# Where the modulation sums of a hybrid encoder layer are worked: all of them ahead of the mLSTM stage

## The chip, the cores and the metric

The kernel runs on one core of a Trainium2 chip. The metric is the device time of one execution in microseconds (us). The core's engines work side by side, each through its own instructions in a fixed order: PE (TensorE, the matrix engine), DVE (VectorE), ACT (ScalarE), POOL (GpSimd) and SP (SyncE), which here does nothing but issue transfers (DMAs). An instruction whose input is not ready holds up all that stand behind it on the same engine.

## The reference, cut to what matters

The input is `x` (1024 positions of 1024 numbers, float32) and a conditioning vector `c`. One layer is computed:

```python
cond = jax.nn.silu(c)
mod = cond @ w_ada + b_ada                  # 6 x 1024 numbers
sh1, sc1, g1, sh2, sc2, g2 = jnp.split(mod, 6, axis=-1)
h = modulate(rms_norm(x, norm_mix_g), sh1, sc1)
proj = h @ w_in                             # q, k, v of the attention; q|k, v, o, gates of the mLSTM
y_attn = axial_gqa_attention(...)           # 8 heads of 64, 2 key/value heads, axial rope on q and k
y_mem = bidirectional_mlstm(...)            # 4 heads of 128, depthwise convolution on q|k, chunked scan both ways
x = x + g1 * (jnp.concatenate([y_attn, y_mem], -1) @ w_out)
h = modulate(rms_norm(x, norm_ffn_g), sh2, sc2)
x = x + g2 * ((silu(h @ w_gate) * (h @ w_up)) @ w_down)
return rms_norm(x, final_norm_g)
```

The matrix products with the weights are kept close to float32: each operand is split into a rounded part ("hi") and a rest ("lo"), and a product is three matmuls, hi*hi, hi*lo and lo*hi.

## The kernel before

**Stages.** In order of time: the load of `x` and the first part of `mod`; the first columns of the input projection; the attention; the mLSTM; the output projection; the feed-forward network (FFN). The tiles have 128 partitions. A product of the input projection has an output of 128x512 or 128x256 that is summed over eight k-tiles of three matmuls each (`mm3`, lines 323 to 325: `acc` for feature-major outputs, `acct` for token-major ones).

**What sets the order.** The program is written out by a planner at build time. `Clock` holds a modelled time, `Engine` adds a modelled cost for every instruction, `ck.chain` runs a list of steps each when the one before is modelled as done, and `Flag` marks an event. `ck.streams(mains, fills, stop)` puts the next ready piece of the main streams on PE, and where none is ready a piece of the fill. During the attention the mains are `scores`, `turned` and `values`, and the fill is the rest of the input projection (`IN`). During the mLSTM the mains are `ends`, `backs`, `fronts` and `all_states`; the fill is first what is left of `IN`, then `MIX`, the output projection: 16 units "o" that read the attention's result (`ya_d`) and 16 units "m" that read the mLSTM's. A unit is 12 matmuls of 128x512 (`acc<-yah`, `yal`). With it come one split of a weight on ACT and DVE (`whi`, `wlo`) and one addition onto `x` on DVE (`x<-acc,mod,x`).

**The modulation sums.** `mod` has 48 columns, each a sum over `w_ada` times `cond`. The first 16 are worked at the start. For the other 32, `ada_late` loads half a column tile at a time (128x512, 64 halves in all, two tiles in turn) and sums it. Halves 0 to 47 are worked in the attention: `scores` calls `ada_late` once a round, the product is made on POOL and the sum on ACT (`ada<-ada,cond`, then `ada,modacc<-ada`). Halves 48 to 63 are worked in the mLSTM stage, where `ck.tick` calls `ada_late` ahead of each piece: product and sum in one instruction on DVE. For these `cond` is loaded and put through its activation a second time (`load_cond`), since the pool that held it has been closed. The list `summed` says that all 64 are added into `mod`. The streams of the first part of the mLSTM stage stop only when the fill `IN` has run out, its outputs are stored and `summed` is set; only then is the pool of `x1` opened, are the rows of `x` loaded, and does `MIX` become the fill.

**The ropes.** `rope_steps` takes one tile of q or k through its normalisation (`ms`, lines 798 and 805), a swap of partitions by four transfers (`sw`), and the rotation. Calls 4 (the keys), 0 and 1 come first; call 1 is the third. `rope_ok[i]` is set when tile i is stored. The keys' rope waits for `rope_ok[0]` and `rope_ok[1]` before its last step. The attention begins (`ready`) when tile 3 is stored and the gates are through.

**Raw weights.** `load_piece` takes the next piece of weights. `piece` sends its load ahead; how far ahead is 2 (`AHEAD`) in part of the list and 0 in the rest.

Of the kernel before, what the change touches and what calls it, by code (L numbers as in the profile page):

```python
# [15 lines left out]
OP = mybir.AluOpType  # L16
# [244 lines left out]
def layer_kernel(ctx, tc, xT, c, w_ada, vecs, cons, rope, w_f, w_fT, w_t0, w_t, w_o, w_gu, w_d, out):  # L261
# [114 lines left out]
    with tc.manual_schedule():  # L376
# [122 lines left out]
        def load_piece():  # L499

            i = len(pieces)
            if i == len(specs):
                return
            while len(made) <= min(i + (AHEAD if i + AHEAD >= start["down"] or start["q", 2] <= i < start["f", 4] else 0), len(specs) - 1):
                piece(len(made))
            p, there, st = made[i]
            pieces.append(p)
            if isinstance(specs[i][0], str):
                set_piece(p, *specs[i][1])
                return  # L510
            split(p, 0.0, lambda: st[0], [P, *specs[i][1:3]], there,
                  lo=dve if i >= start["down"] or i < 12 or start["o", 0] <= i < start["b", 1] else None)
# [247 lines left out]
        def rope_steps(i, accs, raw=None, qg=None):  # L760
# [18 lines left out]
            def rooted(n):  # L779
                dve.tensor_mul(qg[:, halves(n)], accs[n][0], rstd[n])  # L780
                accs[n][1].set(ck, ck.fin + LAT)
# [6 lines left out]
            def swap():  # L788
                sw = X["sw"] = bp.tile([P, S], F32, tag="big", name="sw")
                for b in range(4):  # L790
                    arrive = dma(sw[32 * b:32 * b + 32], qg[32 * (b ^ 1):32 * (b ^ 1) + 32])
                ck.chain(arrive, rp_ok, lambda: dve.tensor_mul(sw, sw, rp[1]), lambda: dve.tensor_mul(qg, qg, rp[0]),
                         lambda: dve.tensor_add(qg, qg, sw), *((*rs_ok, *rope_ok[0:2]) if is_k else ()), finish, store)

# [41 lines left out]
            if raw is None:  # L836
                ck.chain(0.0, lambda: evac(0), lambda: evac(1), swap,
                         *[(slot("ms"), lambda n=n: squares(n)) for n in range(NH if is_k else 1)])
            else:
                ck.chain(0.0, rstd_ok[0], lambda: rooted(0), rstd_ok[1], lambda: rooted(1), shift_ok,  # L840
                         shifted, swap,
                         *[(slot("ms"), lambda n=n: squares(n)) for n in range(NH if is_k else 1)])
# [288 lines left out]
        adas = []  # L1131
        summed = []

        def ada_late(last=48, ahead=2):

            n = len(adas)
            if n == 64 and all(f.done for f in adas[-2:]) and not summed:
                summed.append(1)
                mod_sum(40, 48)
            if n >= last or n >= ahead and not (adas[n - ahead].done and adas[n - ahead].t <= ck.t):  # L1140
                return
            j, i = 16 + n // 2, n % 2
            t = PP["ada"].tile([P, HALF], F32, tag="ada", name="ada", bufs=ahead)
            if n < 48:
                adas.append(ck.chain(dma(t, w_ada[j][:, halves(i)]), lambda: gps.tensor_mul(t, t, PP["cond"][:, halves(i)]),
                                     lambda: act.activation(t, t, AF.Copy, accum_out=modacc[:, i, j:j + 1]),
                                     bg=["gps", "act"]))
                return
            adas.append(ck.chain(dma(t, w_ada[j][:, halves(i)]), lambda: dve.scalar_tensor_tensor(
                t, t, 1.0, PP["cond"][:, halves(i)], op0=OP.mult, op1=OP.mult, accum_out=modacc[:, i, j:j + 1])))  # L1150

# [49 lines left out]
        def turned():  # L1201

            for it in range(NQ // 2):
                for i in range(2):
                    q = 2 * it + i
                    for b in range(2):
# [14 lines left out]
                        if b == 1:  # L1221
                            Tem[q].set(ck, ck.t)

        def values():
# [978 lines left out]
        def ready():  # L2203
            return rope_ok[3].done and logf_ok.done and not open_sum[0]

        ck.streams([un], stop=ready)
        ck.need(*k2_ok, *va_ok)
        stpool.__exit__(None, None, None)
# [6 lines left out]
        ck.streams([un], stop=lambda: convs[-1].done and len(convs) == 8 and not open_sum[0])  # L2215
        while len(adas) < 48:
            ck.need(*adas[-2:])
            ada_late()
# [9 lines left out]
        def mod_sum(a, b):  # L2228
            dve.tensor_add(mod[:, a:b], modacc[:, 0, a:b], V("b_ada", a, b - a))
            dve.tensor_add(mod[:, a:b], mod[:, a:b], modacc[:, 1, a:b])  # L2230

        mod_sum(16, 40)
        sc2 = const.tile([P, KT], F32, name="sc2")
# [11 lines left out]
        load_q(0)  # L2245
        load_cond(bp)
        loaded = [Flag() for _ in range(MH)]
# [3 lines left out]
        mem = [Stream(g) for g in (ends(), backs(), fronts(), all_states())]  # L2251
        ck.tick = lambda: all(f.done for f in heads[0]["in"]) and ada_late(64)
        ck.streams(mem, [un], stop=lambda: un.wait is None and all(f.done for v in vo_ok for f in v) and summed)
        while not summed:
            ck.need(*adas[-2:])
            ada_late(64)
        ck.tick = None
        BIGP[0].__exit__(None, None, None)
# [115 lines left out]
```

## Time and profile before

| | us |
|---|---|
| median of 3 runs (1345.16 to 1345.59) | 1345.42 |
| the profiled execution | 1345.81 |
| its span on the core | 1344.0 |
| PE busy in it | 1276.7 |
| DVE busy in it | 1049.8 |

The span is 1.8 us shorter than the execution's own time; that part lies around the program. By the timeline the attention's first scores are followed by the last product of values at 490.8 us, the mLSTM's first matmuls stand at about 500 us, the first matmul of the output projection at 560.7 us, the mLSTM's last transposes at 624.2 us, and the first matmul of the FFN at 684.5 us. To read the views: "busy" is the time in which an engine had at least one instruction running; PEclk is the clock granted to PE as a share of the full one; a number in square brackets is the time the engine stood idle just before the instruction, and what ended it.

### The profile page before, as it was taken

The numbers are of one execution on the slowest core, as the hardware profiler recorded it, in microseconds if no ns is written. First come the engines' busy times: TensorE is split into PE (matmuls) and PEld (weight loads), VectorE is DVE, ScalarE is ACT, GpSimd is POOL, SyncE is SP. The second block draws the span as 40 slices with busy tenths as digits, with TensorE's granted clock in tenths as the row PEclk, the third lists the DMA queues.
The fourth block names the chain that finished last, engine by engine and source line by source line (L and its number), as shares of the span: only waits on it lengthen the run. The fifth ranks groups of instructions, "written<-read, shape, count | busy, mean of one in ns | idle before, by whom it ended". The sixth has DMA issues, their size and how long they took to land.

```text
span 1344.0 us, 19732 instructions
## 1 busy us (share of the span) xinstructions
PE 1276.7 (95%) x6656; PEld 1080.6 (80%) x6656; DVE 1049.8 (78%) x1694; ACT 707.0 (53%) x1338; POOL 527.7 (39%) x449
## 2 busy tenths in 40 slices
PE   9998898999999998899999999999999999999997
PEld 7887777888888897677878788888888887788886
DVE  7956698778898747997689989867767655888886
ACT  6583566687777756464477432333233333454452
POOL 0071577466676426442135155545454530000002
PEclk9997999899999999999999999999999999999999
DMA  9545433233333226753563344332233258933315
GB/s 374 198 121 141 118 101 107 81 105 90 100 105 103 68 86 212 238 187 126 173 196 102 103 145 146 125 110 102 103 118 107 65 176 303 336 102 95 94 56 164
DMA packets 104613, 187.57 MB, mean 140 GB/s; under 512 B 11584, under 2 KB 33216, under 8 KB 104512
## 3 DMA queue, kind: packets, MB, share of 16 engines
q1 hardware_dynamic: 91264, 164.34, 38.8%
q10 hardware_dynamic: 13248, 21.97, 4.3%
q8 instruction: 53, 0.87, 0.3%
q14 instruction: 48, 0.39, 0.1%
HBM read 139.86 MB, written 42.73 MB: 136 GB/s over the span
## 4 chain that ended last, share of the span: by engine, by line
PE 64%; DVE 14%; issue 8%; POOL 5%; DMA 4%; ACT 4%; SPq 0%; DVEq 0%; ACTq 0%; POOLq 0%
PE acc L325 17%; PE acc L323 17%; PE acc L324 17%; PE av L1233 3%; DVE y L102 2%; PE T L1213 2%; DVE x L102 2%; DVE sst L102 2%; PE S L1181 2%; DVE PT L102 1%; POOL hl L102 1%; POOL P L102 1%; PE acct L323 1%; PE acct L325 1%; PE acct L324 1%
## 5 line engine op out<-in xcount | busy, mean ns | idle before, releaser
L102 ACT ACTIVATE whi<-wst 128x512 fp32r<-128x512 f32 (+2 forms) x223 | 134.0, 607 | 143.0 <-PE acc L325 60.7
L102 POOL TENSOR_TENSOR wlo<-wst,whi 128x512 fp32r<-128x512 f32 x80 | 121.7, 1527 | 150.5 <-ACT whi L102 96.8
L324 PE MATMUL acc<-x,whi 128*128 128x512 f32 x352 | 136.9, 389 | 0.0
L102 POOL TENSOR_SCALAR P<-P,sst 128x1024 f32<-128x1024 f32 x64 | 85.0, 1329 | 93.4 <-DVE sst L102 76.2
L102 DVE TENSOR_TENSOR wlo<-wst,whi 128x512 fp32r<-128x512 f32 (+2 forms) x143 | 93.2, 656 | 30.7 <-ACT whi L102 30.3
L102 DVE TENSOR_TENSOR PT<-T,PT 128x512 fp32r<-128x512 f32 x128 | 84.7, 682 | 23.4 <-ACT PT L102 22.9
L102 POOL TENSOR_TENSOR wlo<-wr,whi 128x512 fp32r<-128x512 f32 x52 | 72.3, 1390 | 71.7 <-ACT whi L102 67.8
L102 POOL TENSOR_TENSOR x<-x,ny 128x256 f32<-128x256 f32 (+1 forms) x8 | 8.3, 1067 | 234.5 <-PE acc L325 214.5
L323 PE MATMUL acc<-hh,whi 128*128 128x512 f32 x224 | 94.3, 421 | 5.5 <-ACT xp L102 4.9
L325 PE MATMUL acc<-whi,wcl 128*128 128x512 f32 x244 | 95.8, 393 | 2.1 <-DVE wcl L102 2.1
L323 PE MATMUL acc<-whi,wch 128*128 128x512 f32 x244 | 95.8, 392 | 1.8 <-ACT wch L102 1.8
L324 PE MATMUL acc<-wlo,wch 128*128 128x512 f32 x244 | 95.6, 392 | 0.0
L324 PE MATMUL acc<-hl,whi 128*128 128x512 f32 x224 | 89.0, 397 | 0.3 <-DVE hl L102 0.3
L325 PE MATMUL acc<-hh,wlo 128*128 128x512 f32 x224 | 89.1, 398 | 0.1
L102 ACT ACTIVATE P<-S,sst,colq 128x1024 f32<-128x1024 f32 x64 | 77.1, 1205 | 21.0 <-DVE sst L102 18.8
L102 ACT ACTIVATE whi<-wr 128x512 fp32r<-128x512 f32 x56 | 35.4, 632 | 100.3 <-DVE wr L102 48.3
L102 ACT ACTIVATE PT<-T 128x512 fp32r<-128x512 f32 x128 | 73.9, 596 | 24.6 <-PE T L1213 23.5
L323 PE MATMUL acct<-whi,hh 128*128 128x256 f32 (+1 forms) x256 | 79.8, 312 | 5.3 <-ACT vstg L102 4.3
L1213 PE MATMUL T<-ident,P 128*128 128x128 f32 x512 | 74.0, 277 | 11.3 <-DVE PT L102 10.2
L102 DVE TENSOR_REDUCE sst<-S 128x1 f32<-128x1024 f32 x64 | 77.7, 1215 | 7.2 <-PE S L1181 7.2
L102 POOL TENSOR_TENSOR ada<-ada,cond 128x512 f32<-128x512 f32 x48 | 72.5, 1512 | 15.9 <-DMA ada<-in_w_ada_dram 15.7
L324 PEld LDWEIGHTS acc<-x,whi 128*128 128x128 f32 x352 | 66.1, 188 | 13.6
(482 smaller groups left out, 3855.3 us busy)
## 6 DMA issues: line engine op xcount, KB each, us to landing
wr<-in_w_gu_dram SPq DMA_DIRECT2D x66, 256.0 KB, 2.9
ada<-in_w_ada_dram SPq DMA_DIRECT2D x64, 256.0 KB, 3.3
wd<-in_w_d_dram SPq DMA_DIRECT2D x22, 512.0 KB, 6.7
wst<-in_w_gu_dram SPq DMA_DIRECT2D x42, 256.0 KB, 3.1
wst<-act_d SPq DMA_DIRECT2D x33, 256.0 KB, 3.6
ada<-in_w_ada_dram SPq DMA_DIRECT2D x16, 512.0 KB, 7.4
wst<-in_w_o_dram SPq DMA_DIRECT2D x32, 256.0 KB, 3.5
act_d<-sg ACTq DMA_DIRECT2D x29, 256.0 KB, 2.2
```

Of the source, the lines that this page charges most:

```text
L102: return fn(*args, **kw)
L323: nc.tensor.matmul(acc, w[0], x[0], start=first, stop=False)
L324: nc.tensor.matmul(acc, w[0], x[1], start=False, stop=False)
L325: nc.tensor.matmul(acc, w[1], x[0], start=False, stop=last)
L1181: nc.tensor.matmul(sp[:, halves(n)], qs[:, j * P:(j + 1) * P], k2[g][m][:, halves(n)], start=m == 0, stop=m == 1)
L1213: nc.tensor.transpose(tp[:, k], Pt[q][:, (4 * b + k) * P:(4 * b + k + 1) * P], ident)
L1233: nc.tensor.matmul(av, va[:, k, h // 4], PT[it, b][m][:, k - 4 * b], start=(k, m) == (0, 0), stop=(k, m) == (NJ - 1, 1))
```

## The change

- `ada_late` works halves in two ways. While the list `calm` is not empty, a half is one instruction on DVE; that holds for the stretch between the first products of the projection and the attention, where `ck.tick` now calls it ahead of each piece on PE. From the start of the attention on it is POOL and ACT.
- In the attention it is called from `scores`, as before, and from `turned` too. All 64 halves are worked by the attention's end, and `mod_sum(16, 48)` adds them in one go. `summed`, the second `load_cond` and the tick of the mLSTM stage are gone, and `MIX` follows as soon as `IN` has run out and is stored.
- The third rope waits for `rope_ok[0]` before its shift; the keys' rope no longer waits for `rope_ok[1]`.
- Raw weights are loaded two pieces ahead up to `start["t", 2]`, which is three conv units (f4, f1, f5) further than before.

```diff
-            while len(made) <= min(i + (AHEAD if i + AHEAD >= start["down"] or start["q", 2] <= i < start["f", 4] else 0), len(specs) - 1):
+            while len(made) <= min(i + (AHEAD if i + AHEAD >= start["down"] or start["q", 2] <= i < start["t", 2] else 0), len(specs) - 1):
...
-                         lambda: dve.tensor_add(qg, qg, sw), *((*rs_ok, *rope_ok[0:2]) if is_k else ()), finish, store)
+                         lambda: dve.tensor_add(qg, qg, sw), *((*rs_ok, rope_ok[0]) if is_k else ()), finish, store)
...
-                ck.chain(0.0, rstd_ok[0], lambda: rooted(0), rstd_ok[1], lambda: rooted(1), shift_ok,
+                ck.chain(0.0, rstd_ok[0], lambda: rooted(0), rstd_ok[1], lambda: rooted(1), shift_ok, *rope_ok[0:i][:1] if i == 1 else (),
                          shifted, swap,
...
-        summed = []
-
-        def ada_late(last=48, ahead=2):
+
+        calm = [True]
+
+        def ada_late(ahead=2):
             n = len(adas)
-            if n == 64 and all(f.done for f in adas[-2:]) and not summed:
-                summed.append(1)
-                mod_sum(40, 48)
-            if n >= last or n >= ahead and not (adas[n - ahead].done and adas[n - ahead].t <= ck.t):
+            if n == 64 or n >= ahead and not (adas[n - ahead].done and adas[n - ahead].t <= ck.t):
                 return
             j, i = 16 + n // 2, n % 2
             t = PP["ada"].tile([P, HALF], F32, tag="ada", name="ada", bufs=ahead)
-            if n < 48:
-                adas.append(ck.chain(dma(t, w_ada[j][:, halves(i)]), lambda: gps.tensor_mul(t, t, PP["cond"][:, halves(i)]),
-                                     lambda: act.activation(t, t, AF.Copy, accum_out=modacc[:, i, j:j + 1]),
-                                     bg=["gps", "act"]))
+            if calm:
+                adas.append(ck.chain(dma(t, w_ada[j][:, halves(i)]), lambda: dve.scalar_tensor_tensor(
+                    t, t, 1.0, PP["cond"][:, halves(i)], op0=OP.mult, op1=OP.mult, accum_out=modacc[:, i, j:j + 1]),
+                    bg=["dve"]))
                 return
-            adas.append(ck.chain(dma(t, w_ada[j][:, halves(i)]), lambda: dve.scalar_tensor_tensor(
-                t, t, 1.0, PP["cond"][:, halves(i)], op0=OP.mult, op1=OP.mult, accum_out=modacc[:, i, j:j + 1])))
+            adas.append(ck.chain(dma(t, w_ada[j][:, halves(i)]), lambda: gps.tensor_mul(t, t, PP["cond"][:, halves(i)]),
+                                 lambda: act.activation(t, t, AF.Copy, accum_out=modacc[:, i, j:j + 1]),
+                                 bg=["gps", "act"]))
...
                             Tem[q].set(ck, ck.t)
+                            ada_late()
...
+        ck.tick = ada_late
         ck.streams([un], stop=ready)
+        ck.tick = None
+        calm.clear()
...
-        while len(adas) < 48:
+        while len(adas) < 64:
             ck.need(*adas[-2:])
             ada_late()
...
-        mod_sum(16, 40)
+        mod_sum(16, 48)
...
-        load_cond(bp)
...
-        ck.tick = lambda: all(f.done for f in heads[0]["in"]) and ada_late(64)
-        ck.streams(mem, [un], stop=lambda: un.wait is None and all(f.done for v in vo_ok for f in v) and summed)
-        while not summed:
-            ck.need(*adas[-2:])
-            ada_late(64)
-        ck.tick = None
+        ck.streams(mem, [un], stop=lambda: un.wait is None and all(f.done for v in vo_ok for f in v))
```

The planner turns this into other orders on every engine. Three places show it.

**PE ahead of the attention.** `ms` are the sums of the ropes' normalisation, in two banks that are used in turn; `acc<-hh,whi` are matmuls of the input projection, and 128x2 x8 is a block of eight small matmuls for one tile of q. Before:

```order
L323 MATMUL acc<-hh_228,whi 128x512
L324 MATMUL acc<-hl_236,whi 128x512
L325 MATMUL acc<-hh_228,wlo 128x512
L805 MATMUL ms<-con,sqk 128x2 x8
L798 MATMUL ms<-sqk,con 128x512
L805 MATMUL ms<-con,sqk 128x2 x8
L323 MATMUL acc<-hh_229,whi 128x512
```

With the change:

```order
L805 MATMUL ms<-con,sqk 128x2 x8
L323 MATMUL acc<-hh_228,whi 128x512
L324 MATMUL acc<-hl_236,whi 128x512
L325 MATMUL acc<-hh_228,wlo 128x512
L805 MATMUL ms<-con,sqk 128x2 x8
L323 MATMUL acc<-hh_229,whi 128x512
```

Three sums stood in a row on PE; now the 128x512 sum is 31 rows ahead of these, and a triple of the projection stands between the two small blocks.

**DVE.** Before, in the mLSTM stage (`num`, `W`, `Cs`, `hs` are its tiles):

```order
L102 SCALAR_TENSOR_TENSOR num<-ni,cols,num 128x130 x2
L102 SCALAR_TENSOR_TENSOR W<-tr,W 128x256 x2
L102 SCALAR_TENSOR_TENSOR ada,modacc<-ada,cond 128x512
L102 SCALAR_TENSOR_TENSOR Cs<-Cs,dec,U 128x130
L102 TENSOR_TENSOR hs<-hs,hs_5877 128x512
```

With the change, ahead of the attention (`raw_q_260` and `qg` are tiles of q in their ropes):

```order
L102 TENSOR_TENSOR sw<-sw,rps 128x1024
L102 SCALAR_TENSOR_TENSOR ada,modacc<-ada,cond 128x512
L102 TENSOR_TENSOR raw_q_260<-raw_q_260,rps 128x1024
L102 SCALAR_TENSOR_TENSOR ada,modacc<-ada,cond 128x512
L102 TENSOR_TENSOR raw_q_260<-raw_q_260,sw 128x1024
```

The 16 sums of the mLSTM stage are gone from DVE, and nine stand among the ropes and the first taps of the convolution. The other 55 are on POOL and ACT, all in the attention, where 48 were.

**PE in the mLSTM stage**, at the place where `IN` has run out. Before:

```order
L1977 LDWEIGHTS identb
L1977 MATMUL E<-maskb,identb 128x512
L1979 MATMUL E<-R,selr 128x256 x2
L1993 MATMUL tr<-mq,mk 128x128 x2
L2024 MATMUL ni<-Cs,mq 128x260
L2019 MATMUL na<-v_5443,W 128x130 x2
L1912 MATMUL tr<-ident,mk 128x128 x2
L1940 MATMUL U<-wv,kt 128x260
```

With the change:

```order
L1979 MATMUL E<-R,selr 128x256 x2
L1993 MATMUL tr<-mq,mk 128x128 x2
L323 MATMUL acc<-yah,whi 128x512
L324 MATMUL acc<-yal,whi 128x512
L325 MATMUL acc<-yah,wlo 128x512
L2024 MATMUL ni<-Cs,mq 128x260
L2019 MATMUL na<-v_5470,W 128x130 x2
```

Before, the mLSTM's matmuls stood alone there; now triples of the output projection stand between them. Of the 384 matmuls of the output projection, 132 stood ahead of the mLSTM's last transposes (`tr<-ident,hs`), and now 222 do. Two smaller shifts go with it: 30 matmuls of 128x512 of the projection pass from ahead of the attention's first scores into the attention, and 33 of 128x256 pass from the attention to behind it. From the point at which 162 matmuls of the output projection are left, PE's rows are the same in both to the program's end.

## The prediction

> **What bounds the kernel now.** I read the page's head and its chain first, then a table of busy times by stage, then the timeline of PE at the gaps, then the groups of DVE in the stage with the largest gap. The head and the chain:
>
> ```profile
> span 1344.0 us, 19732 instructions
> PE 1276.7 (95%) x6656; PEld 1080.6 (80%) x6656; DVE 1049.8 (78%) x1694; ACT 707.0 (53%) x1338; POOL 527.7 (39%) x449
> PE 64%; DVE 14%; issue 8%; POOL 5%; DMA 4%; ACT 4%; SPq 0%; DVEq 0%; ACTq 0%; POOLq 0%
> ```
>
> PE sets the end. The change alters no matmul, so it can move the time only through PE's 67 us of idleness (1344.0 - 1276.7) and through time at a lower clock. Busy time by stage (start:end, length, then PE, PEld, DVE, ACT, POOL, the clock granted to PE, and the DMA's share and rate):
>
> ```profile
> 100.00:157.00 57.00, 52.21 (x235) 42.85 (x235) 34.44 (x50) 22.34 (x37) 14.50 (x13) 0.88 0.44 120
> 157.00:250.00 93.00, 78.66 (x468) 67.96 (x469) 79.63 (x96) 57.95 (x108) 66.82 (x44) 0.96 0.35 103
> 250.00:492.00 242.00, 232.59 (x1576) 208.85 (x1574) 196.07 (x330) 184.06 (x367) 142.53 (x111) 1.00 0.30 89
> 492.00:517.00 25.00, 22.42 (x166) 21.00 (x167) 6.70 (x22) 13.47 (x34) 13.19 (x29) 1.00 0.77 244
> 517.00:560.70 43.70, 32.75 (x190) 27.12 (x189) 41.43 (x132) 25.07 (x74) 23.43 (x41) 0.96 0.57 181
> 560.70:624.20 63.50, 60.81 (x328) 51.27 (x327) 60.66 (x160) 33.24 (x88) 24.03 (x36) 0.97 0.57 190
> 624.20:684.00 59.80, 58.23 (x257) 47.71 (x256) 40.27 (x61) 31.13 (x51) 8.72 (x6) 1.00 0.51 165
> ```
>
> The fifth row is the place: from 517 to 560.7 us PE idles 10.95 of 43.7 us while DVE is busy for 95% of it. There the mLSTM has PE to itself, because the output projection may start only when the sums are done. Once it may (sixth row), PE idles 2.69 of 63.5 us. PE at both ends of that stretch (start, duration, instruction, in brackets the idle time before it):
>
> ```profile
> 550.34 0.60 PE L2024 MATMUL ni<-Cs,mq 128*128 128x260 f32 x2
> 554.15 0.99 PE L2088 MATMUL tr<-ident,hs 128*128 128x128 f32 x4 [3.20 <-DVE W L102]
> 554.93 1.07 PE L2019 MATMUL na<-v,W 128*128 128x130 f32 x4
> ...
> 560.74 0.58 PE L323 MATMUL acc<-yah,whi 128*128 128x512 f32 x1
> 561.16 0.39 PE L324 MATMUL acc<-yal,whi 128*128 128x512 f32 x1
> 561.38 0.39 PE L325 MATMUL acc<-yah,wlo 128*128 128x512 f32 x1
> ...
> 624.16 0.60 PE L2088 MATMUL tr<-ident,hs 128*128 128x128 f32 x4
> 626.32 0.50 PE L323 MATMUL acc<-yah,whi 128*128 128x512 f32 x1 [1.56 <-DVE yal L102]
> ```
>
> **The mLSTM stage.** What leaves DVE and what comes to it, from DVE's groups between 515 and 620 us (busy us, mean ns of one):
>
> ```profile
> L102 DVE SCALAR_TENSOR_TENSOR ada<-ada,cond 128x512 f32<-128x512 f32 x14 | 9.7, 692 | 0.0
> L102 DVE TENSOR_TENSOR wlo<-wst,whi 128x512 fp32r<-128x512 f32 x11 | 7.8, 713 | 0.0
> L102 DVE SCALAR_TENSOR_TENSOR x<-acc,mod,x 128x512 f32<-128x512 f32 x9 | 6.7, 743 | 0.0
> L102 DVE DVE_READ_ACCUMULATOR ada<-ada,cond 128x1 f32 x14 | 1.1, 78 | 0.0
> ```
>
> Fourteen sums go (9.7 + 1.1 = 10.8 us; two more stand ahead of 515). In the new order 90 more matmuls of the output projection stand ahead of the last transposes, that is 7.5 units: seven additions and eight weight splits, 7 x 0.743 + 8 x 0.713 = 10.9 us. So DVE's load in the stage stays: 41.43 + 60.66 = 102.1 us from 517 to 624.2. PE's load grows. Two matmuls of a triple start 0.22 to 0.23 us apart (561.16 to 561.38), so the 90 are 20.5 us, and they no longer stand behind 624.2. The gain is thus what PE's idleness swallows of 20.5 us.
>
> PE's losses in the 107.2 us are 10.95 + 2.69 us idle, and by the clock 0.04 x 43.7 + 0.03 x 63.5 = 3.6 us: 17.2 in all, so full-speed work is 90.0, and with the projection 110.5. Were nothing lost, the stage would take 110.5 and the gain be 107.2 + 20.5 - 110.5 = 17.2 us. If it loses at the rate of the stretch that already has the projection beside it, (2.69 + 1.9) / 63.5 = 7.2%, it takes 119.1, gain 8.6. In that stretch DVE was 96% busy; with 102 us of work in some 116 it would be at 88%, and the gaps that DVE ended there should shrink. I take 4.7% and a gain of 11 us, and keep 8.6 and 17.2 as bounds. The cover would be gone if the mLSTM's chain waited for PE itself, which is a rival below. Behind 624.2 nothing pays it back: PE's rows there are the same, and DVE, busy for 40.27 of 59.8 us, has room for its part. The second `cond` goes too, and the SP queue loses the stage's 16 loads; PE idles 2.6 us from 492 to 517, of which I take nothing.
>
> **Ahead of the attention.** PE at the sums of the ropes:
>
> ```profile
> 112.60 1.84 PE L805 MATMUL ms<-con,sqk 128*128 128x2 f32 x16
> 114.30 1.10 PE L798 MATMUL ms<-sqk,con 128*128 128x512 f32 x2
> 119.22 3.57 PE L805 MATMUL ms<-con,sqk 128*128 128x2 f32 x16 [3.82 <-DVE rqv L102]
> 123.23 0.63 PE L324 MATMUL acc<-hl,whi 128*128 128x512 f32 x1
> 123.66 0.63 PE L325 MATMUL acc<-hh,wlo 128*128 128x512 f32 x1
> ...
> 128.49 0.40 PE L324 MATMUL acc<-hl,whi 128*128 128x512 f32 x1
> 128.73 0.39 PE L325 MATMUL acc<-hh,wlo 128*128 128x512 f32 x1
> ```
>
> The third sum finds both banks taken and waits 3.82 us. Behind it PE runs at half speed for a while: the same block takes 3.57 instead of 1.84 us, and some nine matmuls start 0.43 us apart (123.23 to 123.66) instead of 0.24 (128.49 to 128.73). That is 3.82 + 1.73 + 9 x 0.2 = 7.4 us. In the new order the third rope comes later and the sums have triples between them, with 30 matmuls (7 us) behind the 128x512 one, so no bank is waited for. What comes late instead is tile 1 of q, which only the attention's third head reads. I take 6 us of 7.4, with nothing as the other bound: the wait could come back at the block that now stands a triple behind its fellow. [...]
>
> The nine sums now on DVE here cost 9 x (0.692 + 0.078) = 6.9 us. DVE is idle for 57 - 34.4 = 22.6 us of this stretch, so I cost them at nothing; if they all stood in its way it would be 6.9. The longer lookahead only moves six loads of weights ahead of the time they are due; I cost it at nothing.
>
> **The attention.** Seven pairs more on POOL and ACT, from the tile's own rows (min/median/max ns):
>
> ```profile
> L328 SPq DMA_DIRECT2D ada<-in_w_ada_dram x80: 327/333/1202, 1.6 to 550.5; - x80
> L102 POOL TENSOR_TENSOR ada<-ada,cond x48: 1266/1295/3272, 167.1 to 446.9; 128x512 f32<-128x512 f32 x48
> L102 ACT ACTIVATE ada<-ada x48: 617/632/650, 169.3 to 449.9; 128x512 f32<-128x512 f32 x48
> L102 ACT ACTIVATION_READ_ACCUMULATOR ada<-ada x48: 184/192/219, 169.8 to 450.4; 128x1 f32 x48
> ```
>
> Seven times 1.3 us on POOL is 9 us, and 7 x 0.82 = 5.8 us on ACT. POOL is busy for 66.82 + 142.53 = 209 of 335 us, ACT for 242, so most is hidden; I take 1.5 us lost, between nothing and 9. The 33 and 30 matmuls that change sides run on PE either way. The loads on SP stay 80; only their places move, at about 0.33 us of the queue each.
>
> **The sum**: 1345.8 (the profiled execution) - 11 - 6 + 1.5 = 1330.3, and 0.4 less against the median of the runs, 1345.4: 1330 us.
>
> **The rivals.** *The mLSTM waits for PE in turn* (15%). Its matmuls and its DVE steps alternate; groups of three to twelve projection matmuls (0.7 to 2.7 us) now stand ahead of them in PE's order. If each such group delays the chain by its whole length, the stage grows by the 20.5 us that leave its end, and only the front gains: 1345.4 - 6 + 1.5 = 1341. Against it speaks the sixth row, where such groups stand already and PE still idles.
>
> *All idleness is covered* (10%): 17.2 + 7.4 us less, 1321. DVE at 88% speaks for it, the alternation against.
>
> *The wait ahead of the attention moves* (8%): the front gains nothing, say because the delayed third rope holds a bank at the end of it, and 11 - 1.5 remain: 1336.
>
> *POOL and DVE stretch the attention* (8%), which ends slower than before. From 157 to 250 us DVE is busy for 79.63 of 93 us and POOL for 66.82, and they slow each other:
>
> ```profile
> 153.07 3.98 DVE L102 SCALAR_TENSOR_TENSOR y<-xp,vec,y 128x1024 f32<-128x1024 f32 x3
> 162.59 9.06 DVE L102 SCALAR_TENSOR_TENSOR y<-xp,vec,y 128x1024 f32<-128x1024 f32 x4
> 160.65 1.29 POOL L102 TENSOR_TENSOR wlo<-wst,whi 128x512 fp32r<-128x512 f32 x1 [9.71 <-DMA qd<-q_d]
> 167.10 2.16 POOL L102 TENSOR_TENSOR ada<-ada,cond 128x512 f32<-128x512 f32 x1
> ```
>
> Three taps take 1.33 us each while POOL is idle (the 9.71 us ahead of its row at 160.65), four take 2.27 each beside its work from there on. If the attention's rounds come to be bound there, the nine sums on DVE count at twice their price (13.8), the seven pairs on POOL in full (9), and the five taps of the convolution that the new order puts behind the first scores' maximum at 0.94 us more each (4.7): 27.5 us against the gain of 17, so 1345.4 + 10.5 = 1356. It decides from the point where the rounds, not PE, set the pace in most of the attention; in the third row PE is busy for 96% of its time, which speaks against it. [...]
>
> The forecast itself keeps 59%.
>
> **How the numbers follow.** The range takes the forecast's bounds (front 0 to 7.4, mLSTM 8.6 to 17.2, attention 0 to 9): from 1345.4 - 24.6 = 1321 to, with the middle of the attention's, about 1341, which takes in the second to fourth case; I put it at 1319 to 1342, leaving the slow rival and the corners outside. A measurement of this kernel tells 0.2% (2.7 us) from no change. Faster: the forecast and the cases at 1321 and 1336, 77%, and of the case at 1341 half, since its 4.4 us are near what can be told: 85%. The other half, 7%, is within 0.2%, and slower is the last rival's 8%.
>
> **What would show it.** Right: in the changed profile no wait of `ms` on `rqv` near 115 us and a clock near 1 from 110 to 130; the first `acc<-yah` some 40 us earlier than 560.7; PE idle for 5 us or less, not 13.6, between there and the last transposes; and those followed by 162 matmuls only. Wrong: long gaps of PE in that stretch ended by `W` or `num`; an attention (first scores to last `av`) in which PE's idle time grows by more than 5 us; or the last transposes later than 635 us.

## The result, and the profile after

| | us |
|---|---|
| kernel before, beside it (1345.16 to 1347.31) | 1345.51 |
| changed kernel, median of 4 runs (1332.32 to 1333.89) | 1332.91 |
| ratio, with its 95% interval | 0.9904 (0.9887 to 0.9922) |

The changed kernel is faster by 12.6 us; 1330 was forecast. The page's head and its chain of the changed kernel:

```profile
span 1331.3 us, 19726 instructions
PE 1269.8 (95%) x6648; PEld 1074.7 (81%) x6656; DVE 1051.7 (79%) x1678; ACT 706.0 (53%) x1349; POOL 532.6 (40%) x456
PE 67%; DVE 14%; ACT 5%; DMA 4%; issue 4%; POOL 4%; SPq 0%; ACTq 0%; DVEq 0%; POOLq 0%
```

PE still sets the end. It is busy for 6.9 us less with the same matmuls, so part of the gain is time at a lower clock (the mean granted clock is 0.986 before and 0.991 after), and idle for 61.5 us instead of 67.3. How the gain splits between the two is known to some 2 us only: a second profile of the changed kernel, taken for the experiments, has PE busy for 4.6 us less and idle for 59.0 us. To see where, I cut both spans at the same events: the start, the attention's first scores, its last product of values, the mLSTM's last transposes, the FFN's first matmul, the end. Busy time by stage (columns as in the prediction), before:

```profile
0.00:168.00 168.00, 155.32 (x778) 128.94 (x779) 118.32 (x196) 99.73 (x170) 46.10 (x42) 0.96 0.58 191
168.00:491.60 323.60, 303.74 (x2012) 271.06 (x2011) 267.25 (x421) 235.24 (x465) 202.81 (x150) 0.99 0.31 91
491.60:624.16 132.56, 116.24 (x683) 99.44 (x682) 108.75 (x310) 71.84 (x193) 60.64 (x104) 0.97 0.61 197
624.16:684.52 60.36, 58.80 (x260) 48.15 (x258) 40.83 (x62) 31.65 (x52) 8.72 (x6) 1.00 0.50 164
684.52:1344.00 659.48, 642.64 (x2929) 533.00 (x2927) 514.68 (x708) 268.51 (x459) 209.42 (x148) 0.99 0.42 137
```

and after:

```profile
0.00:157.60 157.60, 146.05 (x748) 122.12 (x748) 124.03 (x211) 98.25 (x169) 46.04 (x38) 0.98 0.64 213
157.60:488.40 330.80, 307.02 (x2008) 272.67 (x2009) 271.69 (x424) 239.67 (x479) 217.29 (x160) 0.98 0.32 96
488.40:634.10 145.70, 138.16 (x798) 118.28 (x805) 112.70 (x291) 74.54 (x203) 55.80 (x107) 0.99 0.51 165
634.10:673.40 39.30, 38.36 (x170) 31.14 (x168) 30.32 (x47) 24.86 (x41) 3.79 (x3) 1.00 0.58 186
673.40:1331.30 657.90, 640.17 (x2929) 530.50 (x2927) 512.99 (x708) 268.68 (x459) 209.72 (x148) 1.00 0.41 137
```

Lengths can't be compared as they stand, since matmuls changed sides: the counts show 30 fewer ahead of the attention (778 to 748) and 90 fewer behind the last transposes (260 to 170). Thirty of 128x512 at 0.228 us (their starts in PE's timeline lie 0.22 to 0.24 us apart) are 6.85 us that left the first stage for the second; 33 of 128x256 at 0.12 us (their distance in PE's timeline) are 4.0 us that left the second for the third; ninety at 0.228 are 20.5 us that left the fourth for the third.

| stage | length before, after | work moved | gain | forecast |
|---|---|---|---|---|
| ahead of the attention | 168.0, 157.6 | -6.85 | 3.5 | 6 |
| attention | 323.6, 330.8 | +6.85 - 4.0 | -4.3 | -1.5 |
| mLSTM | 132.6, 145.7 | +4.0 + 20.5 | 11.4 | 11 |
| rest of the output projection | 60.4, 39.3 | -20.5 | 0.6 | 0 |
| FFN | 659.5, 657.9 | 0 | 1.6 | 0 |

The FFN's matmuls are the same in every kernel of this study, and its length went from 656.5 to 661.7 us in their profiles: the last row is scatter. The first rows scatter too. In four profiles that share everything up to the attention's end (the changed kernel twice, and the first two experiments below) the first scores come at 157.6, 157.8, 159.6 and 157.6 us, which puts the front's gain between 1.6 and 3.5 us, and the attention takes 330.6 to 331.5 us. In the experiments I therefore give, beside the time, the moment of the FFN's first matmul in the profile. It is 684.5 before and 673.4 after.

**The mLSTM stage** is what it was foretold to be. PE's rows at its two ends:

```profile
520.53 0.47 PE L323 MATMUL acc<-yah,whi 128*128 128x512 f32 x1
...
634.10 0.60 PE L2088 MATMUL tr<-ident,hs 128*128 128x128 f32 x4
634.45 0.48 PE L323 MATMUL acc<-yah,whi 128*128 128x512 f32 x1
```

The output projection starts 40.2 us earlier than at 560.74. What PE waits for in the stage (total us, times, longest), before:

```profile
PE tr L2088 <- DVE W L102: 7.2, 3, 3.2
PE ni L2024 <- DVE num L102: 4.0, 6, 1.3
PE tr L1912 <- DVE W L102: 1.7, 1, 1.7
```

and after:

```profile
PE ni L2024 <- DVE num L102: 4.7, 6, 2.8
PE tr L1993 <- DMA mq<-mqk_d: 1.7, 1, 1.7
```

The waits for `W`, 8.9 us, are gone; those for `num` stayed.

**Ahead of the attention** the old wait is gone and another has come. PE's sums of the ropes, after:

```profile
109.85 1.84 PE L805 MATMUL ms<-con,sqk 128*128 128x2 f32 x16
112.33 1.84 PE L805 MATMUL ms<-con,sqk 128*128 128x2 f32 x16
131.95 3.45 PE L805 MATMUL ms<-con,sqk 128*128 128x2 f32 x16 [5.12 <-ACT sqk L102]
```

The first two blocks run without a wait at full speed (1.84 us each, clock 1.00). The block of the last rope (tile 3 of q) waits 5.12 us for `sqk`, which ACT makes, and runs at half speed behind it (3.45 us; the clock is 0.50 from 132.16 to 138.99). Why ACT is late stands in ACT's own timeline and in the SP queue's:

```profile
117.59 1.06 ACT L102 ACTIVATE k<-kdup 128x1024 fp32r<-128x1024 f32 x1 [2.68 <-DMA kdup<-raw_q]
125.68 1.06 ACT L102 ACTIVATE k<-kdup 128x1024 fp32r<-128x1024 f32 x1 [7.03 <-DMA kdup<-raw_q]
```

```profile
113.30 8.94 SPq L328 DMA_DIRECT2D kdup<-raw_q  x4
```

`kdup` holds the rotated keys of one key head in both halves of its partitions; there are two such tiles, with two transfers each. They come from the same ring of three buffers (`row_tile`, tag "raw") as the raw tiles of q. The ring held a tile of the third rope, which the change makes late, so the second tile had to wait for the first one to come free: the four issues are spread over 8.94 us of the queue. The third of them starts at 121.1 us, when POOL has read the first tile (its row at 118.72 takes 2.39 us). ACT stood 7.03 us at the copy, with the evacuations of the last rope queued behind it, and PE waited for those.

### The profile page after: what moved, and what is told of

The parts are those of the page before. It is cut to its first block, busy times and chain, and to the rows that moved or that the text cites. A ratio compares the mean times of both kernels' runs of the same rounds, so it can differ in the third digit from the quotient of the medians.

```text
span 1331.3 us, 19726 instructions
## 1 busy us (share of the span) xinstructions
PE 1269.8 (95%) x6648; PEld 1074.7 (81%) x6656; DVE 1051.7 (79%) x1678; ACT 706.0 (53%) x1349; POOL 532.6 (40%) x456
## 4 chain that ended last, share of the span: by engine, by line
PE 67%; DVE 14%; ACT 5%; DMA 4%; issue 4%; POOL 4%; SPq 0%; ACTq 0%; DVEq 0%; POOLq 0%
PE acc L325 17%; PE acc L323 17%; PE acc L324 17%; PE av L1233 3%; PE T L1212 3%; DVE x L102 3%; PE S L1180 2%; DVE sst L102 2%; POOL wlo L102 1%; DVE PT L102 1%; PE acct L323 1%; DVE wlo L102 1%; DVE y L102 1%; PE acct L325 1%; PE acct L324 1%
## 5 line engine op out<-in xcount | busy, mean ns | idle before, releaser
L1212 PE MATMUL T<-ident,P 128*128 128x128 f32 x512 | 74.5, 278 | 15.7 <-DVE PT L102 11.7
L102 POOL TENSOR_TENSOR ada<-ada,cond 128x512 f32<-128x512 f32 x55 | 82.1, 1498 | 15.5 <-DMA ada<-in_w_ada_dram 15.2
L1212 PEld LDWEIGHTS T<-ident,P 128*128 128x128 f32 x512 | 59.6, 143 | 23.9 <-POOL P L102 8.3
```

The costliest lines, as they stand in the source:

```text
L102: return fn(*args, **kw)
L1212: nc.tensor.transpose(tp[:, k], Pt[q][:, (4 * b + k) * P:(4 * b + k + 1) * P], ident)
```

## The experiments

All times are medians. The kernels ran in three groups, each on one chip beside runs of the kernel before. Those gave 1344.81 for the first group (the gate, the refill, the copy in another ring, the ropes undone), 1344.03 for the second (the changed kernel again, no pairs, no sums on DVE, the lookahead undone) and 1343.13 for the last (the four kernels with the copy free). Executions scattered more than before (1338.25 to 1348.47 in the first group), so ratios of different groups tell no more than about 0.2% apart. Where two parts are varied in one kernel, the edit is the two diffs shown for them.

### What pays in the mLSTM stage: relief of DVE, or an earlier fill

One kernel keeps all sums ahead of the stage, but holds the output projection back to about the point where the kernel before could start it. The other starts it early, but loads DVE again with sixteen sums on a spare tile.

```diff
-        ck.streams(mem, [un], stop=lambda: un.wait is None and all(f.done for v in vo_ok for f in v))
+        GATE = ck.t + 57.75
+        ck.streams(mem, [un], stop=lambda: un.wait is None and all(f.done for v in vo_ok for f in v) and ck.t >= GATE)
```

> The changed kernel, but the output projection may begin only as late in the planner's time (57.75 us behind the stage's start) as in the kernel before; DVE stays relieved of the 16 sums. If what gained in the mLSTM stage is the early fill (theory), PE idles there for about 12 us again and the time is 1341 to 1345. If it is the 10.8 us that left DVE (rival), the mLSTM alone runs faster, PE's idle time stays near 5 us and the time is 1333 to 1336.

```diff
+        spare = mp.tile([P, HALF + 1], F32, name="spare")
+        gps.memset(spare, 0.0)
+        refill = []
+        FROM = ck.t + 12.0
+
+        def refilled():
+            dve.scalar_tensor_tensor(spare[:, 0:HALF], spare[:, 0:HALF], 1.0, spare[:, 0:HALF], op0=OP.mult, op1=OP.mult,
+                                     accum_out=spare[:, HALF:HALF + 1])
+
+        def again_dve():
+            if ck.t > FROM and len(refill) < 16 and all(f.done for f in refill[-1:]):
+                refill.append(ck.chain(2.2, refilled))
+
+        ck.tick = again_dve
```

> The changed kernel with 16 products and sums of 128x512 put back on DVE in the mLSTM stage (on a spare tile, nothing loaded, result unused); the output projection still begins early. Theory (the early fill): DVE has 108.3 + 10.8 us of work in a stage of 121 us, it fits nearly, and the time is 1333 to 1337. Rival (DVE's load): the whole mLSTM gain of 11 us goes, 1342 to 1345.

Measured: with the gate 1340.33 us (1338.22 to 1343.28), ratio 0.9974 (0.9955 to 0.9992), first FFN matmul at 680.9; with DVE refilled 1342.36 (1339.87 to 1347.79), ratio 0.9991 (0.9969 to 1.0013), at 681.9. The gate's time lies between its two expected ranges, the refill's in that of its rival. The two intervals overlap and that of the refill contains 1, so the times say only that each kernel loses most of the gain; the split below rests on one profile of each. Busy time from the start of the output projection to the last transposes, with the gate:

```profile
558.11:620.56 62.45, 59.94 (x320) 49.60 (x321) 57.91 (x149) 32.97 (x88) 22.49 (x34) 1.00 0.55 186
```

with DVE refilled:

```profile
518.95:642.69 123.74, 115.42 (x591) 95.50 (x597) 112.49 (x294) 62.53 (x167) 44.36 (x72) 0.94 0.48 153
```

and in the changed kernel:

```profile
520.53:634.10 113.57, 108.40 (x578) 90.14 (x583) 104.06 (x266) 60.58 (x163) 39.71 (x70) 0.98 0.49 160
```

From the last product of values to the FFN the kernel before takes 192.9 us. Less the 4.0 us that moved in, the changed kernel takes 181.0, a gain of 11.9; the gate leaves 185.9, a gain of 7.0; the refilled DVE 189.8, a gain of 3.1. So neither half is the whole. (The gate's first scores came at 159.6 us, 2 us later than in the changed kernel, with nothing edited ahead of them; counting from the last product of values leaves that out.) Relief of DVE gives the larger part by itself, although PE then has nothing to fill its gaps with. The early fill with DVE loaded as before gives little, since DVE's 8.4 us more in the stretch come back as length and as a clock of 0.94. By these rows DVE sets the pace here: it is busy for 112.5 of 123.7 us, and its 8.4 us more went with 10.2 us more of length.

### The wait ahead of the attention

The two tiles of the copy are taken from another ring; the order of the instructions on every engine stays.

```diff
-                    t = row_tile("kdup")
+                    t = stp.tile([P, S], F32, tag="x", name="kdup", bufs=KT)
```

> The changed kernel, in which the two copies of the keys take tiles of the x ring instead of the ring of three that the late third rope still holds; the order on every engine is the same. Theory: PE's new wait of 5.12 us near 127 us and the half speed behind it come from the second copy waiting for the first one's tile, with SP and ACT held behind it; the first scores come 5 to 8 us earlier and the time is 1325 to 1330. Rival: PE waits because the third rope's own transfers come late, so the wait stays and the time is 1332 to 1334.

Measured: 1329.23 us (1327.34 to 1330.95), ratio 0.9894 (0.9857 to 0.993). The SP queue and PE in that kernel:

```profile
113.16 3.06 SPq L328 DMA_DIRECT2D kdup<-raw_q  x4
```

```profile
128.40 1.84 PE L805 MATMUL ms<-con,sqk 128*128 128x2 f32 x16
...
152.28 3.50 PE L1180 MATMUL S<-k,qs 128*128 128x512 f32 x8 [3.94 <-POOL qs L102]
```

Four issues span 3.06 us instead of 8.94, the wait of 5.12 us is gone, and the first scores come at 152.3 instead of 157.6. This settles the cause of the wait. The FFN starts at 669.1 instead of 673.4.

The same kernel ran once more in the last group, beside three that vary it.

> The changed kernel with the second copy of the keys in a tile of its own, once more, beside the kernels that vary it. Theory (the copy waited for a tile that the late third rope held; that wait cost 3 to 5 us of the front, of which the attention gives 1 to 2 back): first scores near 152.3 us, PE idle near 8.4 us ahead of them, time 1328 to 1331. Rival (the earlier 1329.2 against 1332.9 was scatter between executions): 1331.5 to 1334.

Measured: 1330.58 us (1328.55 to 1332.85), ratio 0.9906 (0.9888 to 0.9925); first scores at 151.5, PE idle 7.3 us ahead of them, FFN at 669.4. The profile repeats to a microsecond: 4 us earlier at the FFN. The ratio does not show them, since 0.9906 is that of the changed kernel; what the copy's wait costs the whole time is at the edge of what these runs tell.

### The ropes' order undone, with the copy held and with it free

```diff
-                         lambda: dve.tensor_add(qg, qg, sw), *((*rs_ok, rope_ok[0]) if is_k else ()), finish, store)
+                         lambda: dve.tensor_add(qg, qg, sw), *((*rs_ok, *rope_ok[0:2]) if is_k else ()), finish, store)
...
-                ck.chain(0.0, rstd_ok[0], lambda: rooted(0), rstd_ok[1], lambda: rooted(1), shift_ok, *rope_ok[0:i][:1] if i == 1 else (),
+                ck.chain(0.0, rstd_ok[0], lambda: rooted(0), rstd_ok[1], lambda: rooted(1), shift_ok,
```

> The changed kernel with the ropes as before: the third waits for nothing, the keys' one for tiles 0 and 1. Theory: the old wait of 3.82 us near 115 us and its half speed (7.4 us together) return and the new wait of 5.12 us goes, nearly even: 1332 to 1336. Rival: the ropes' order is worth the 6 us of the forecast: 1338 to 1340.

Measured, the changed kernel with this alone: 1329.72 us (1328.03 to 1333.47), ratio 0.9902 (0.9872 to 0.9932), FFN at 672.3. The time lies below both expected ranges. The old wait is back with 2.08 us, and the first scores come 1.9 us later, at 159.5, but the attention takes 328.0 us instead of 330.8 (0.7 of that is six matmuls of 128x256 that left it). The new order of the ropes is worth nothing in the change as it was made.

> The copy in a tile of its own, and the ropes waiting for one another as in the kernel before. If the new order of the ropes is worth something once the copy is out of its way: the third block of sums waits for rqv again (2.1 to 3.8 us), PE idles 11 to 13 us ahead of the first scores instead of 8.4, and the time is 2 to 4 us above the copy alone, 1331 to 1334. If the new order is worth nothing even then: idle time ahead of the first scores within 1.5 us of the copy alone, time within 1.5 us of it.

Measured, with the copy free as well: 1328.82 us (1326.49 to 1336.0), ratio 0.99 (0.9877 to 0.9923), FFN at 671.3. Here my expectation failed in its second half. The front is worse, and more so than foretold: PE idles 14.1 us ahead of the first scores, which come at 163.0. Yet the FFN starts only 1.8 us later, and the time is not above that of the copy alone. The front and the attention in the kernel with the copy alone:

```profile
0.00:151.50 151.50, 144.17 (x749) 120.59 (x749) 124.44 (x211) 99.35 (x169) 46.46 (x39) 0.99 0.66 222
151.50:484.10 332.60, 309.47 (x2008) 274.83 (x2009) 274.01 (x424) 238.62 (x479) 214.31 (x160) 0.97 0.31 96
```

and with the ropes undone too:

```profile
0.00:163.00 163.00, 148.88 (x748) 123.57 (x748) 119.79 (x212) 98.66 (x170) 47.88 (x39) 0.95 0.63 208
163.00:487.50 324.50, 306.27 (x2003) 269.98 (x2004) 267.85 (x423) 236.53 (x476) 205.12 (x159) 0.99 0.32 97
```

With the same matmuls ahead of the first scores, a front that is 11.5 us longer goes with an attention that is 8.1 us shorter. Six matmuls of 128x256 (0.7 us) have left the attention, PE idles 4.9 us less in it, and the clock is 0.99 instead of 0.97. PE's rows around the first scores show part of the exchange. With the copy alone:

```profile
151.46 3.05 PE L1180 MATMUL S<-k,qs 128*128 128x512 f32 x8 [3.26 <-POOL qs L102]
155.76 2.07 PE L1180 MATMUL S<-k,qs 128*128 128x512 f32 x4 [1.25 <-ACT P L102]
159.46 1.97 PE L1212 MATMUL T<-ident,P 128*128 128x128 f32 x8 [1.62 <-POOL P L102]
```

with the ropes undone:

```profile
163.05 3.78 PE L1180 MATMUL S<-k,qs 128*128 128x512 f32 x8 [6.30 <-POOL qs L102]
```

The one waits 3.3 us ahead of the first scores and 2.9 more just behind them for `P`; the other waits 6.3 ahead of them and 0.16 in the 12 us behind. That the attention's start has a chain of its own, which is waited for on the one side of the first scores or on the other, fits these rows; it is argued, not shown by a run of its own. It can't be all: from 90 to 150 us behind the first scores PE idles 7.7 us in the kernel with the copy alone and 2.8 with the ropes undone, and that is far behind these rows. That stretch returns below.

### The attention's 4.3 us: is it the pairs?

The changed kernel once more, then a kernel that leaves the 55 pairs of products and sums in the attention out (its `mod` lacks them), then one that has all 64 there and none on DVE.

> The changed kernel once more, as the measure for the others of this call: 1330 to 1335.

Measured: 1332.98 us (1332.47 to 1333.29), ratio 0.9918 (0.9903 to 0.9932), FFN at 672.9.

```diff
+    nc.gpsimd.memset(modacc, 0.0)
...
+            if not calm:
+                adas.append(FREE)
+                return
```

> The changed kernel without the 55 loads and sums of the attention (this part of mod is left out, so the numbers that come out are others; nothing else is left out). The attention, from the first scores to the last product of values, takes 330.8 us in the changed kernel and 323.6 before, of which 2.9 are moved matmuls. Theory: the pairs on POOL and ACT are what lengthens it; without them it takes 320 us or less and the time is 1318 to 1324. Rival: DVE's taps at its start do it; it stays at 328 to 331 and the time is 1329 to 1333.

Measured: 1336.22 us (1334.71 to 1338.88), ratio 0.9938 (0.9922 to 0.9955), FFN at 679.5.

```diff
-        ck.tick = ada_late
+        calm.clear()
         ck.streams([un], stop=ready)
-        ck.tick = None
-        calm.clear()
```

> The changed kernel without sums on DVE ahead of the attention: all 64 on POOL and ACT in it. Theory (the nine on DVE are hidden, pairs in the attention are not): the first scores come within 1 us of 157.6, the attention grows by 3 to 6 us, 1334 to 1338. Rival (the nine sums on DVE delay the ropes and taps): first scores 2 to 4 us earlier and the time is 1329 to 1332.

Measured: 1332.72 us (1329.43 to 1335.32), ratio 0.9915 (0.9896 to 0.9934), FFN at 672.5. Neither expectation of these two kernels held: without pairs the attention takes 322.5 us, between the two, and the kernel slows; without sums on DVE the first scores come at 161.5 (18 matmuls more stand ahead of them) and the attention is 7.2 us shorter, not longer. Busy time in the attention, without pairs:

```profile
159.70:482.20 322.50, 299.90 (x1945) 264.92 (x1946) 265.11 (x422) 203.76 (x363) 126.00 (x103) 0.98 0.17 50
```

with 64 pairs:

```profile
161.50:485.10 323.60, 305.38 (x2048) 273.07 (x2047) 267.31 (x421) 242.73 (x495) 218.95 (x166) 1.00 0.34 104
```

PE idles 22.6 us there without any pair, 19.9 with 48 (before), 23.8 with 55 (after) and 18.2 with 64. The idleness does not go with the number of pairs, on POOL's load from 126 to 219 us. Without pairs the attention holds 63 matmuls of 128x256 fewer than in the changed kernel; at 0.12 us they are 7.6 of the 8.3 us by which it is shorter. So the pairs are not what costs. The kernel without them is slower than the changed one: the planner, with other costs, spread the fill in another way, and the output projection opened at 552.5 us instead of 520.5. The gate's kernel, which opened at 558.1, was late by as much, so this is the likely reason; as a test of the pairs by the whole time the run is inconclusive.

### The lookahead undone, and the two that beat both kernels

```diff
-            while len(made) <= min(i + (AHEAD if i + AHEAD >= start["down"] or start["q", 2] <= i < start["t", 2] else 0), len(specs) - 1):
+            while len(made) <= min(i + (AHEAD if i + AHEAD >= start["down"] or start["q", 2] <= i < start["f", 4] else 0), len(specs) - 1):
```

> The changed kernel with the lookahead of raw weights as before. Theory: worth nothing, within 2 us of the changed kernel. Rival: the loads two ahead save waits of POOL and ACT on weights at the attention's start: 1335 to 1338.

Measured, the changed kernel with this alone: 1332.13 us (1331.65 to 1332.48), ratio 0.9912 (0.9897 to 0.9926), FFN at 671.1: the time differs by 0.9 us.

> The copy in a tile of its own, and the lookahead of raw weights as in the kernel before. Theory (the lookahead is worth nothing by itself; it only shifts which matmuls fill which gaps): time within 2 us of the copy alone, 1327 to 1331, PE idle in the attention lower by some us and the clock or the mLSTM stage taking it back. Rival (the longer lookahead makes weights ready in time): PE waits for wst or whi in the attention, 3 us or more slower than the copy alone.

Measured, with the copy free too: 1324.92 us (1323.36 to 1332.66), ratio 0.9873 (0.9849 to 0.9898), FFN at 664.0. This missed the expectation of no more than 2 us: 5.7 lower than the copy alone (1330.58) by the medians, and 5.4 earlier at the FFN. Four of its five runs lie below all of the copy alone, the fifth among them, and the two intervals overlap.

> The copy in a tile of its own, and no modulation sum on DVE ahead of the attention: all 64 pairs are worked on POOL and ACT from the attention's start on. Theory (nine more pairs in the attention cost nothing; the sums on DVE stand between the steps of the last rope and delay the first scores by the 2.5 us of two of them): PE idle ahead of the first scores 2 to 4 us less than with the copy alone, PE idle in the attention no more than 24 us, the mLSTM stage gives some of it back, time 1326 to 1330. Rival (pairs cost the attention 1.3 us each on POOL): PE idle in the attention 9 us more or above 30 us, time 1333 to 1340.

Measured, with the copy free and no sum on DVE ahead of the attention: 1325.28 us (1324.65 to 1326.49), ratio 0.9868 (0.9846 to 0.9889), FFN at 666.0; all four runs are below all five of the copy alone. Of the steps expected, the idle time ahead of the first scores did not fall (7.2 us, with 18 more matmuls before them), but that of the attention did, from 23.1 to 16.6:

```profile
156.90:480.50 323.60, 307.04 (x2049) 274.68 (x2047) 264.82 (x421) 242.59 (x495) 215.73 (x165) 0.99 0.34 103
```

Both beat the kernel before by 1.3%. The nine sums and the longer lookahead, which measured as nothing while the copy was held, measure as 5.3 and 5.7 us by the medians once it is free, and as 3.4 and 5.4 by the start of the FFN. That the copy's wait hid them is not shown. Of PE's idle time ahead of the FFN the undone lookahead takes about as much off in either case: from 42.1 to 39.0 us with the copy held, from 39.1 to 35.8 with it free. Where the gain lies the profiles say (the attention: PE idle 16.6 and 18.6 us instead of 23.1); which instruction's place makes it, and whether the two add up, was not tried.

## Why the prediction was right, and where it was not

**What bounds it.** As read: the stage that the table of busy times named gave 11.4 of the 12.7 us of span.

**The mLSTM stage (-11).** Right in size, and the reasoning holds with one thing made sharper. The working has a slip: by its own sum a loss of 4.7% gives 11.7 us, and 11 would need 5.3%. The loss from 520.5 on, idle time and clock together, measured some 6% in this profile and some 5% in the second one. "DVE's load in the stage stays": from 520.5 on DVE is busy for 104.06 of 113.57 us, against 102.1 foretold; that is 92%, not 88%. "What PE's idleness swallows": PE idles 5.2 us in that stretch, not 13.6 (the sign asked for 5 or less), and the clock is 0.98. The prediction left open how much of this the removed sums buy and how much the early fill. The gate and the refill answer it: 7.0 us by the one alone, 3.1 by the other, 11.9 together. The rival in which the mLSTM waits for PE in turn is refuted: from the last product of values to the last transposes it takes 13.1 us more, with 24.5 us more work in it.

**Ahead of the attention (-6).** The step that failed is "so no bank is waited for". No bank is, but the sentence ends at the banks. "What comes late instead is tile 1 of q, which only the attention's third head reads" overlooked that the late tile also holds a buffer of a ring from which the keys' copy takes its own. The term measured 3.5 us (1.6 to 3.5 over four profiles), and with the ropes undone the whole was no slower. Of the rival "the wait ahead of the attention moves" this is half: the wait did move, to the next rope's block and to another cause, and half of the front's gain went with it. "A clock near 1 from 110 to 130" held in this profile (1.00), not behind the new wait (the row below). In the second profile of the same kernel it is 0.91: the clock stood at 0.50 from 114.8 to 118.2 with no wait ahead of it, right behind the first two blocks of small sums.

```profile
100.00:157.60 57.60, 49.48 (x228) 40.56 (x226) 46.59 (x61) 28.24 (x42) 20.12 (x14) 0.94 0.59 172
```

**Nine sums on DVE (0), lookahead (0).** Both held in the change as it was made: with either undone the time is the same. With the copy free the medians say 5 us for each, near the bound of 6.9 for the sums; for the lookahead I had no bound at all, and the cover that I named for it, loads ahead of the time they are due, was not what counted. Why the two terms show in one kernel and not in the other stays open.

**The attention (+1.5).** It lost 4.3, within the bounds of 0 to 9. The step that failed is the cause: "seven pairs more on POOL and ACT" do not make it, by the kernels with 64 pairs and with none. PE's idle time grew by 3.9 us. Two rows within 8 us of the first scores hold 4.2 of waits for `P`, where the kernel before waited 0.4 for it:

```profile
161.78 1.20 PE L1180 MATMUL S<-k,qs 128*128 128x512 f32 x4 [2.04 <-ACT P L102]
...
165.14 1.97 PE L1212 MATMUL T<-ident,P 128*128 128x128 f32 x8 [2.17 <-POOL P L102]
```

That this nearly equals the loss is chance, since a larger one stands later. From 90 to 150 us behind the first scores PE idles 8.3 us, where it idled 1.4 before:

```profile
258.00:318.00 60.00, 58.57 (x377) 51.44 (x376) 46.85 (x81) 51.72 (x110) 40.08 (x35) 1.00 0.34 103
```

```profile
247.60:307.60 60.00, 51.69 (x364) 46.87 (x363) 44.90 (x75) 47.35 (x100) 37.58 (x29) 0.97 0.29 91
PE T L1212 <- DVE PT L102: 7.3, 4, 3.1
```

Four waits of transposes for `PT`, the copy that DVE makes of the transposes before, are 7.3 us of it; the stretches from 30 to 90 us and from 150 to 240 us give 6.3 back. The same stretch idles 7.7 to 8.3 us in all six profiles in which ropes, sums, pairs and lookahead stand as in the change, with the copy held or free; 4.4 in the one without pairs; and 2.0 to 2.9 in all six in which ropes, sums or lookahead are undone. So it comes with one order that the planner wrote and is tied to no single part; which instruction makes it was not tried.

The prediction added the front's gain and the attention's loss as if each stood for itself. Every part moved the order behind it: with the copy free, the kernel whose first scores come 11.5 us later starts the FFN only 1.8 us later, and in this stretch alone PE idles 4.9 us less there.

**The sum.** Foretold were 15.5 us, 12.7 came in the span: the front gave 2.5 less, the attention took 2.8 more, the mLSTM 0.4, the rest of the projection 0.6 and the FFN's scatter 1.6 the other way.

## What to carry to other kernels

When a step is made late to free one resource, list every resource that it holds: here a bank was freed and a tile of a shared ring was held instead, and the time over which the queue's four issues for one copy are spread (8.94 us, against 3.06) showed it. Where a planner writes the order, undoing one part writes a new order everywhere behind it, so a part that measures as nothing in one kernel can measure as 5 us in another; try it again once the others have changed, and look for waits that come and go with parts that have nothing to do with them. Where work changes sides of a cut, compare stages only after taking the moved work out.

## What was not expected of the hardware

**The clock after short waits.** The same block of sums, behind a wait of the same length, ran at full speed in one kernel and at half speed in another. With the ropes undone:

```profile
118.73 1.92 PE L805 MATMUL ms<-con,sqk 128*128 128x2 f32 x16 [2.08 <-DVE rqv L102]
```

with the ropes undone and the copy free:

```profile
119.84 3.35 PE L805 MATMUL ms<-con,sqk 128*128 128x2 f32 x16 [2.08 <-DVE rqv L102]
```

The clock fell in both, 3.0 us behind the wait's end in the first and 0.2 us behind it in the second (columns as before):

```profile
118.73:121.72 2.99, 2.99 (x21) 2.81 (x22) 2.49 (x10) 0.88 (x3) 0.00 (x0) 1.00 0.98 327
121.72:125.13 3.41, 3.41 (x9) 2.67 (x8) 3.41 (x6) 0.00 (x0) 0.00 (x0) 0.50 0.67 226
```

```profile
116.64:120.05 3.41, 1.33 (x7) 0.81 (x6) 2.34 (x5) 2.23 (x6) 1.17 (x1) 1.00 0.51 115
120.05:126.88 6.83, 6.83 (x25) 6.06 (x25) 4.90 (x14) 0.66 (x3) 0.00 (x0) 0.50 0.74 252
```

In the kernel before, a wait of 3.51 us that ended at 160.05 was followed by no fall: the clock is 1.00 over the next 10 us. So the length of a wait alone does not tell whether the clock falls. Its place tells more, by the profiles of the kernel before and of the changed one. In both the changes of the granted clock lie whole multiples of 3.41 us apart. Cut into such pieces, the wait of 2.08 us in the second kernel lies whole in one (the third row above, PE busy 1.33 of 3.41 us), and the wait of 3.51 us lies in two, with 1.78 and 1.73 us idle. Of the pieces at full clock in these two profiles, up to PE's last matmul, all seven with 2.0 us idle or more were followed by half clock, three of the ten with 1.6 to 2.0 us, and one of the 741 with less, which holds the ropes' small sums at 101.61 in the kernel before. That is a count over profiles that were made for other ends, not a test.

**A sum on DVE beside POOL.** The prediction priced a sum at 0.69 us plus 0.08. With the copy in a tile of its own, DVE's timeline has

```profile
137.39 1.78 DVE L102 SCALAR_TENSOR_TENSOR ada<-ada,cond 128x512 f32<-128x512 f32 x1
...
140.24 0.68 DVE L102 SCALAR_TENSOR_TENSOR ada<-ada,cond 128x512 f32<-128x512 f32 x1
```

and POOL's

```profile
137.05 1.57 POOL L102 TENSOR_TENSOR wlo<-wst,whi 128x512 fp32r<-128x512 f32 x1 [0.68 <-ACT whi L102]
```

Beside a weight split on POOL that began 0.34 us earlier the sum takes 2.6 times as long as alone (1.78 us; 0.68 at 140.24, where no instruction of POOL runs). It need not: in the changed kernel's own profile a sum and a split start together at 144.01, and there the sum takes 0.68 us and the split 1.83, where the median of such splits on POOL is 1.30.
